# Memory keys of the sample group: from 128x128 turns on TensorE to 32x32 turns on VectorE, with scores in 32x32 tiles

## The chip, the cores and the metric

The kernel runs on one core of a Trainium2 chip. The metric is the time of one execution on the device in microseconds; the kernel before is stated by the median of its runs, and one further execution was profiled.

## What is computed

One layer of a hybrid decoder, for a prompt of 512 rows and a sample group of 8 sequences with 4 rows each, with the same weights: a mixer (mLSTM and differential attention), a cross-attention into 256 memory tokens, and a gated feed-forward part with a short convolution. The change lies in the cross-attention of the sample group. Its keys and values come from caches, 256 tokens by 4 heads by 256 features for each sequence:

```python
def mem_attend(h, mk, mv, w_mq, w_mo):
    B, T, _ = h.shape
    q = (h @ w_mq).reshape(B, T, MEM_HEADS, MEM_HEAD_DIM)
    s = jnp.einsum('bqhd,bkhd->bhqk', q.astype(jnp.float32), mk.astype(jnp.float32)) * (MEM_HEAD_DIM ** -0.5)
    p = jax.nn.softmax(s, axis=-1)
    o = jnp.einsum('bhqk,bkhd->bqhd', p, mv.astype(jnp.float32)).reshape(B, T, D_MODEL)
    return o.astype(h.dtype) @ w_mo
```

## The kernel before

Rows are worked in blocks of 128 partitions: four blocks of the prompt, and one block of 32 rows (`NS`) for the sample group. Large matrix products take the prompt's weights and activations as two parts each (a rounded part and a rest), three products for each; the sample group is computed in plain f32, which TensorE works off as two records for each product.

The instructions of each engine are in one order, made ahead of time: a scheduler goes through the program as written, and takes an instruction that stands later when an earlier one has to wait for its operands or for a free buffer. Buffers come from pools. The ones that matter here:

- `stg` ("st", 6 buffers of 128x1024 f32): staging for everything that is loaded, weights and cached keys alike.
- `wp` ("W", 4 buffers, each twice as large): weights after their split, the turned keys `kT`, and the cached values `vt`.
- `psm` ("mm", 5 banks) and `psa` ("at", 3 banks): the accumulators of TensorE.
- `zp` (3 buffers) and `t2p` (8 buffers): the prompt's probabilities, and what they become when turned.

The stage that the change touches runs like this. The queries of both groups are projected by `gemmB` in eight blocks of 128 features (`ev_q` takes each out of its bank; block m of the sample group lands in `qs[:, m, :]`). The first four blocks are done with all weights at hand, the last four one after the other, and behind each of these two tiles of 128 cached memory tokens are loaded (`mk_load`) and turned (`mk_turn`): eight transposes of 128x128 on TensorE against the identity (L1387), four to a bank, and each bank is copied to `kT` by ScalarE or VectorE (L1388). Each sequence has two such tiles. A loop over the eight sequences then computes scores (`mk_scores`, L1397): for each of two halves of the features and each head a product with 128 features on the rows, the 32 sample rows as weights, and 256 tokens as moving columns; the four heads stand at partitions 0, 32, 64 and 96 of one bank. `sample_exp` takes a maximum over the 256 tokens (L1014) and an exponential with its sum (L1015). All 32 rows meet all eight sequences; the pairs that don't belong together are masked out later, in `sample_softmax`, which joins the eight results into `az`. The weighted sums (`mv_out`, L1407) go through the cached values, loaded by `mv_load` as one 1 MB transfer a sequence.

The prompt's own cross-attention is a pipeline of eight steps, `prompt`, from which the loop takes a step here and there by `next(prompt)`: `ch_soft` (scores L1338 and their softmax), two steps later `ch_turn` (transposes L1356), one later `ch_out` (L1368, on every second step). It gives TensorE work while the sample group's softmax is under way. `NMID` steps follow the softmax of the sample group and the rest stand between the weighted sums, behind the sequences named in `VSTEPS`. The output weights `w_mo` are loaded through staging buffers into W buffers (`slotsA`), at most four ahead. After them comes the output projection.

Loads go out on SyncE's queue (SP), in the order of its instructions: a load that waits for a free buffer holds up those behind it.

Of the kernel before, what the change touches and what calls it, by code (L numbers as in the profile page):

```python
# [7 lines left out]
F32 = mybir.dt.float32  # L8
# [65 lines left out]
def kernel(ctx: ExitStack, tc: tile.TileContext, I, O):  # L74
    nc = tc.nc
# [25 lines left out]
    def N(name, w=1024):  # L101
        return npool.tile([P, 1032], F32, name=name, tag="N")[:, :w]
# [20 lines left out]
    def v2(t, b):  # L123
        return t.rearrange("p (a b) -> p a b", b=b)

    mm = nc.tensor.matmul
# [28 lines left out]
    ident = con("ident")  # L155
# [49 lines left out]
    def stage():  # L205
        return stg.tile([P, 1024], F32, name="wst", tag="st")
# [806 lines left out]
    def sample_exp(sall, b, ps, nm, su):  # L1013
        VRED(out=nm[:, b:b + 1], in_=ps, axis=AX.X, op=MAX, negate=True)  # L1014
        ACT(out=sall[:, b, :], in_=ps, func=AF.Exp, bias=nm[:, b:b + 1], accum_out=su[:, b:b + 1])  # L1015
# [289 lines left out]
        split(mvN[0][:, c], mvN[1][:, c], st)  # L1305

    qs = sm.tile([P, 8, NS], F32, name="qs", tag="qz", bufs=1)
    qh, ql = [], []

    def ev_q(m):  # L1310
        if m % 2 == 0:
            qh.append(npool.tile([P, 2, 516], F32R, name="qh", tag="N"))
        if m % 4 == 0:
            ql.append(S([P, 4, SEQ], F32R, "ql"))

        def ev(i, c0, c1, ps):
# [3 lines left out]
            STT(out=ql[m // 4][:, m % 4, c0:c0 + n], in0=ps[:, :n], scalar=1.0 / 16.0, in1=f32(q), op0=MUL, op1=SUB)  # L1320
            if i == 1:
                nc.scalar.mul(out=qs[:, m, :], in_=ps[:, n:n + NS], mul=1.0 / 16.0)
        return ev

    run(gemmB(hqT, [ev_q(m) for m in range(4)], half_first=True))
# [3 lines left out]

    def ch_soft(i):  # L1330
        h, bp = i // 2, i % 2
        sv = v2(mmp("sca"), 256)
        for j in range(2):
            t0 = (2 * bp + j) * P
            for c in range(2):
                q, l = qh[h][:, c, t0:t0 + P], ql[h // 2][:, 2 * (h % 2) + c, t0:t0 + P]
                for m, (x, k) in enumerate(((q, 0), (q, 1), (l, 0))):
                    mm(sv[:, j, :], lhsT=x, rhs=mkT[k][:, 2 * h + c, :], start=(c + m == 0), stop=(c == 1 and m == 2))  # L1338
        nm = small(2, "cnm")
        su = small(2, "csu")  # L1340
        VRED(out=nm, in_=sv, axis=AX.X, op=MAX, negate=True)
        p = cps[i] = v2(Z("cp"), 256)
        for j in range(2):
            ACT(out=p[:, j, :], in_=sv[:, j, :], func=AF.Exp, bias=nm[:, j:j + 1], accum_out=su[:, j:j + 1])
        nc.vector.reciprocal(out=su, in_=su)
        for j in range(2):
            VTS(out=p[:, j, :], in0=p[:, j, :], scalar1=su[:, j:j + 1], scalar2=None, op0=MUL)

    def ch_turn(i):
        h, bp = i // 2, i % 2  # L1350
        if bp == 0:
            pTs[h] = [[T2([P, SEQ], "pT", F32R) for _ in range(2)] for _ in range(2)]
        tp = mmp("cpt")
        for c in range(2):
            for j in range(2):
                tr(tp[:, (2 * c + j) * P:(2 * c + j + 1) * P], cps[i][:, j, c * P:(c + 1) * P], ident)  # L1356
        for c in range(2):
            split(*[p[:, 256 * bp:256 * bp + 256] for p in pTs[h][c]], tp[:, 256 * c:256 * c + 256])
# [16 lines left out]
    def mk_load(i):  # L1375
        b, c = i // 2, i % 2
        kst[i] = stage()
        dma(out=kst[i], in_=I["cache_mem_k"][0, b, c * P:(c + 1) * P].rearrange("t h d -> t (h d)"))

    def mk_turn(i):  # L1380
        b, c = i // 2, i % 2
        if c == 0:
            kts[b] = wp.tile([P, 8, 256], F32, name="kT", tag="W")
        for q in range(2):
            ps = at("tpk")
            for j in range(4):
                tr(ps[:, j * P:(j + 1) * P], kst[i][:, (4 * q + j) * P:(4 * q + j + 1) * P], ident)  # L1387
            (VCP if q else nc.scalar.copy)(out=kts[b][:, 4 * q:4 * q + 4, c * P:(c + 1) * P], in_=v2(ps, P))  # L1388

    def mk_scores(i):  # L1390
        b, c = i // 2, i % 2
        if c == 0:
            return
        ps = mmp("ssc")[:, :256]
        for c in range(2):
            for h in range(H):
                mm(ps[NS * h:NS * h + NS], lhsT=qs[:, 2 * h + c], rhs=kts[b][:, 2 * h + c, :], start=(c == 0), stop=(c == 1))  # L1397
        sample_exp(sall, b, ps, nm, su)

    def mv_load(b):  # L1400
        vts[b] = wp.tile([P, 2, DM], F32, name="vt", tag="W")
        dma(out=vts[b], in_=I["cache_mem_v"][0, b].rearrange("(c p) h d -> p c (h d)", p=P))

    def mv_out(b):
        for c in range(2):
            for h in range(H):
                mm(pso[NS * h:NS * h + NS], lhsT=az[c][:, h, b * NS:(b + 1) * NS], rhs=vts[b][:, c, 256 * h:256 * h + 256],  # L1407
                   start=(b == 0 and c == 0), stop=(b == NB - 1 and c == 1))

    sall = S([P, NB, 256], F32, "cas")  # L1410
    nm, su = small(NB, "snm"), small(NB, "ssu")
    prompt = pipe(8, ch_soft, lambda i: None, ch_turn, ch_out)

    for i in range(6):
        mk_load(i)
    for i, _ in enumerate(gemmB(hqT, [ev_q(m) for m in range(4, 8)])):
        if i % 4 == 3:
            for j in (i // 2 - 1, i // 2):
                mk_turn(j)
                mk_load(j + 6)  # L1420
    for b in range(NB):
        mk_scores(2 * b + 1)
        if b < 4:
            for j in (2 * b + 8, 2 * b + 9):
# [380 lines left out]
```

## Time and profile before

| | |
|---|---|
| median of 3 runs | 997.69 us (997.62 to 998.53) |
| profiled execution, its own time | 996.59 us |
| its span, first to last instruction | 994.8 us |
| TensorE busy | 967.3 us |
| VectorE busy | 600.0 us |
| ScalarE busy | 389.0 us |
| GpSimd busy | 194.1 us |
| moved by DMA | 130.26 MB, mean 131 GB/s |
| granted TensorE clock, mean | 0.989 |

Engines are named PE (TensorE's matmuls), PEld (its weight loads, which overlap them), DVE (VectorE), ACT (ScalarE), POOL (GpSimd) and SP (SyncE). A row of a group gives the line, the engine, the operation, the tiles written and read, the shape as partitions by elements, the count, then busy time in us and the mean duration of one in ns, and behind the second bar the idle time of the engine ahead of it with what ended it. For a matmul the shape begins with rows*columns of the array. A matmul's duration counts from its start to a modelled end, and several overlap; what one costs is seen from the length of a run of them. A row of a timeline gives the start, the length, and what ran, with the count. The queue q8 is that of TensorE's instructions.

### The profile page before, as it was taken

The page shows a single profiled execution, that of the slowest core. Times are in us where ns is not written, and L with a number is a line of the kernel's source. Part 1 is how long each engine was busy: PE and PEld are TensorE (multiplying, and loading weights), DVE is VectorE, ACT ScalarE, POOL GpSimd, SP SyncE. Part 2 cuts the span into 40 slices and gives each one's busy share as a digit, 9 for nine tenths or more (in the row PEclk, how much of TensorE's full clock was granted, in tenths as well). Part 3 has the DMA queues.
Part 4 walks back from the last instruction along what each step waited for, and adds up shares of the span by engine and source line. Part 5 has one row for each costly group of instructions (what it writes and reads, how often), then busy time and mean ns, then how long its engine had stood idle before and what let it go on. Part 6 is the DMA issues. An engine that isn't in the chain of part 4 may idle for free.

```text
span 994.8 us, 17056 instructions
## 1 busy us (share of the span) xinstructions
PE 967.3 (97%) x6615; PEld 812.5 (82%) x6615; DVE 600.0 (60%) x1129; ACT 389.0 (39%) x746; POOL 194.1 (20%) x389
## 2 busy tenths in 40 slices
PE   8999999999899999999999999999999999999994
PEld 5899777789555778898767789979987997997983
DVE  5734325643686356743653678827848685675677
ACT  5754323234376447633552444242212222222232
POOL 6610000102332124500000264301101110010115
PEclk9999999999799999999999999999999999999998
DMA  8940222352634167775851673153053213314113
GB/s 289 296 155 1 85 85 88 80 188 60 178 114 145 42 212 237 262 247 165 282 213 43 196 238 107 25 150 94 15 138 88 84 46 102 117 40 132 39 46 111
DMA packets 120401, 130.26 MB, mean 131 GB/s; under 512 B 8423, under 2 KB 85832, under 8 KB 120320
## 3 DMA queue, kind: packets, MB, share of 16 engines
q1 hardware_dynamic: 114136, 125.69, 40.6%
q10 hardware_dynamic: 6184, 3.48, 1.2%
q8 instruction: 52, 0.85, 0.4%
q14 instruction: 29, 0.24, 0.1%
HBM read 112.22 MB, written 16.93 MB: 130 GB/s over the span
## 4 chain that ended last, share of the span: by engine, by line
PE 85%; DVE 6%; DMA 5%; issue 2%; ACT 1%; POOL 1%; SPq 0%; DVEq 0%; POOLq 0%; ACTq 0%
PE mm L455 31%; PE mm L386 6%; PE mm L387 6%; PE mm L388 6%; PE mm L443 5%; PE mm L1647 4%; PE mm L1649 4%; PE mm L1648 4%; PE mm L366 3%; PE sda L1182 2%; DMA xb<-x_d 2%; PE tpk L1387 2%; PE cpo L1368 1%; PE sca L1338 1%; PE ssc L1397 1%
## 5 line engine op out<-in xcount | busy, mean ns | idle before, releaser
L142 ACT CAST wslot<-wst 128x1024 fp32r<-128x1024 f32 (+1 forms) x127 | 131.1, 1036 | 274.5 <-issue 74.4
L455 PE MATMUL mm<-fT,wslot 128*128 128x256 f32 (+1 forms) x1872 | 235.7, 288 | 0.0
L455 PEld LDWEIGHTS mm<-fT,wslot 128*128 128x128 f32 x1872 | 234.7, 188 | 0.7 <-issue 0.4
L143 DVE TENSOR_TENSOR wslot<-wst,wslot 128x1024 fp32r<-128x1024 f32 (+1 forms) x127 | 155.1, 1223 | 92.3 <-ACT wslot L142 91.7
L1647 PE MATMUL mm<-wslot,act 128*128 128x512 f32 (+1 forms) x176 | 71.0, 405 | 0.0
L1648 PE MATMUL mm<-wslot,act 128*128 128x512 f32 (+1 forms) x176 | 69.6, 395 | 0.0
L1649 PE MATMUL mm<-wslot,act 128*128 128x512 f32 (+1 forms) x176 | 69.1, 397 | 0.0
L1548 POOL COPY cvo<-u 128x2 f32<-128x2 f32 x43 | 16.1, 375 | 221.4 <-DVE u L1546 221.4
L386 PE MATMUL mm<-wslot,hT 128*128 128x512 f32 x128 | 51.8, 408 | 0.0
L455 PE MATMUL mm<-hT,wslot 128*128 128x256 f32 (+1 forms) x384 | 51.4, 290 | 0.0
L387 PE MATMUL mm<-wslot,hT 128*128 128x512 f32 x128 | 50.8, 397 | 0.0
L388 PE MATMUL mm<-wslot,hT 128*128 128x512 f32 x128 | 50.6, 398 | 0.0
L455 PEld LDWEIGHTS mm<-hT,wslot 128*128 128x128 f32 x384 | 48.9, 188 | 0.9 <-issue 0.8
L1647 PEld LDWEIGHTS mm<-wslot,act 128*128 128x128 f32 (+1 forms) x176 | 33.4, 190 | 15.8 <-issue 7.8
L1543 DVE TENSOR_TENSOR u<-mm,rsb 128x256 f32<-128x256 f32 x43 | 18.1, 423 | 43.4 <-PE mm L455 43.3
L1649 PEld LDWEIGHTS mm<-wslot,act 128*128 128x128 f32 (+1 forms) x176 | 33.0, 188 | 7.7 <-issue 0.4
L1648 PEld LDWEIGHTS mm<-wslot,act 128*128 128x128 f32 (+1 forms) x176 | 33.1, 188 | 6.4
L1560 ACT ACTIVATE c<-c 128x560 f32<-128x560 f32 x21 | 14.1, 672 | 60.2 <-DVE c L1554 60.2
L1660 DVE TENSOR_TENSOR yp<-mm,yp 128x512 f32<-128x512 f32 x40 | 27.3, 689 | 13.7 <-PE mm L1649 13.6
L1554 DVE SCALAR_TENSOR_TENSOR c<-u,cvT,c 128x560 f32<-128x560 f32 x43 | 34.3, 798 | 0.8
L1553 DVE SCALAR_TENSOR_TENSOR c<-u,cvT,c 128x560 f32<-128x560 f32 x43 | 34.1, 793 | 0.1
L386 PEld LDWEIGHTS mm<-wslot,hT 128*128 128x128 f32 x128 | 24.1, 188 | 6.6 <-issue 2.1
(458 smaller groups left out, 1876.6 us busy)
## 6 DMA issues: line engine op xcount, KB each, us to landing
wst<-in_w_up_dram SPq DMA_DIRECT2D x42, 512.0 KB
wst<-in_w_in_dram SPq DMA_DIRECT2D x28, 512.0 KB
wst<-in_w_down_dram SPq DMA_DIRECT2D x20, 512.0 KB
wst<-in_cache_mem_k_dram SPq DMA_DIRECT2D x16, 512.0 KB
vt<-in_cache_mem_v_dram SPq DMA_DIRECT2D x8, 1024.0 KB
wst<-in_w_mk_dram SPq DMA_DIRECT2D x8, 512.0 KB
xb<-in_x_prompt_dram SPq DMA_DIRECT2D x8, 512.0 KB
wst<-in_cache_dk_dram SPq DMA_DIRECT2D x16, 256.0 KB
```

Source lines behind the costliest of these rows:

```text
L142: nc.scalar.copy(out=hi, in_=src)
L143: (eng or nc.vector).tensor_tensor(out=lo, in0=src, in1=f32(hi), op=SUB)
L386: mm(ps[b], lhsT=xt.hi(k, c0, c0 + n), rhs=s[:, 0, kk, :], start=(k == 0), stop=False)
L387: mm(ps[b], lhsT=xt.hi(k, c0, c0 + n), rhs=s[:, 1, kk, :], start=False, stop=False)
L388: mm(ps[b], lhsT=xt.lo(k, c0, c0 + n), rhs=s[:, 0, kk, :], start=False, stop=(k == nk - 1))
L443: mm(ps, lhsT=s[:, l, k, :], rhs=x(k, c0, c1), start=(k == 0 and j == 0), stop=(k == 7 and j == 2))
L455: mm(ps[i], lhsT=s[:, l, k, :], rhs=x(k, c0, c1), start=(k == 0 and j == 0), stop=(k == 7 and j == 2))
L1553: STT(out=c, in0=u[:, 1:EXT - 1], scalar=w[1], in1=c, op0=MUL, op1=ADD)
L1554: STT(out=c, in0=u[:, 0:EXT - 2], scalar=w[0], in1=c, op0=MUL, op1=ADD)
L1647: mm(ps, lhsT=t[:, 0, c0:c0 + P], rhs=s[:n, 0, i % 2, :], start=st, stop=False)
L1648: mm(ps, lhsT=t[:, 0, c0:c0 + P], rhs=s[:n, 1, i % 2, :], start=False, stop=False)
L1649: mm(ps, lhsT=t[:, 1, c0:c0 + P], rhs=s[:n, 0, i % 2, :], start=False, stop=en)
```

## The change

The tile of 128 tokens by 1024 features is turned by one VectorE instruction, which turns each block of 32x32 in its place. The partitions then hold, in four groups of 32, the features of a block; the columns hold 32 blocks of features, with 32 tokens of the group in each. A product can therefore take 32 features at a time, for 32 tokens of each of two tiles (64 columns). The eight blocks of a head are summed in the bank, and each group of partitions (32 tokens of a tile) has a bank of its own: `sc[g]`, 64 columns for each sequence, held over all eight sequences. The queries must stand on every group of partitions, so `q4` gets 32 small copies from `qs`. The softmax is taken for four sequences at once (`mk_soft`): behind sequence 3, and behind sequence 7. Since four of the five `psm` banks are held, the prompt's scores and transposes move to the `psa` pool. The values of sequences 0, 1, 2 and 7 go into two staging buffers each instead of a W buffer, those of 0 to 6 are loaded inside the loop, and the prompt's steps are taken at other places.

```diff
+    q4 = N("q4").rearrange("p (r m n) -> p r m n", r=4, m=8)
...
                 nc.scalar.mul(out=qs[:, m, :], in_=ps[:, n:n + NS], mul=1.0 / 16.0)
+                if m % 4 == 3:
+                    for r in range(4):
+                        for g in range(4):
+                            cp = (nc.gpsimd.tensor_copy, VCP, nc.gpsimd.tensor_copy, nc.scalar.copy)[g]
+                            cp(out=q4[32 * g:32 * g + 32, r, m - 3:m + 1], in_=qs[32 * r:32 * r + 32, m - 3:m + 1])
...
-        sv = v2(mmp("sca"), 256)
+        sv = v2(at("sca"), 256)
...
-        tp = mmp("cpt")
+        tp = at("cpt")
...
-            kts[b] = wp.tile([P, 8, 256], F32, name="kT", tag="W")
-        for q in range(2):
-            ps = at("tpk")
-            for j in range(4):
-                tr(ps[:, j * P:(j + 1) * P], kst[i][:, (4 * q + j) * P:(4 * q + j + 1) * P], ident)
-            (VCP if q else nc.scalar.copy)(out=kts[b][:, 4 * q:4 * q + 4, c * P:(c + 1) * P], in_=v2(ps, P))
...
+            kts[b] = wp.tile([P, 2, 32, 32], F32, name="kT", tag="W")
+        nc.vector.transpose(out=kts[b][:, c].rearrange("p a b -> p (a b)"), in_=kst[i])
+
+    def mk_scores(b):
+        for j in range(8):
+            for h in range(H):
+                for g in range(4):
+                    gr = slice(32 * g, 32 * g + 32)
+                    mm(sc[g][NS * h:NS * h + NS, 64 * b:64 * b + 64], lhsT=q4[gr, j % 4, 2 * h + j // 4, :],
+                       rhs=kts[b][gr, :, 8 * h + j, :], start=(j == 0), stop=(j == 7))
+
+    def mk_soft(b0):
+        for g in range(4):
+            VRED(out=nm4[:, b0:b0 + 4, g], in_=v2(sc[g][:, 64 * b0:64 * b0 + 256], 64), axis=AX.X, op=MAX, negate=True)
+        VRED(out=nm[:, b0:b0 + 4], in_=nm4[:, b0:b0 + 4, :], axis=AX.X, op=MIN)
+        for b in range(b0, b0 + 4):
+            for g in range(4):
+                ACT(out=v2(sall[:, b, :], P)[:, :, 32 * g:32 * g + 32], in_=v2(sc[g][:, 64 * b:64 * b + 64], 32), func=AF.Exp,
+                    bias=nm[:, b:b + 1], accum_out=su4[:, b, g:g + 1])
+        VRED(out=su[:, b0:b0 + 4], in_=su4[:, b0:b0 + 4, :], axis=AX.X, op=ADD)
+
+    def mv_load(b):
+        src = I["cache_mem_v"][0, b].rearrange("(c p) h d -> c p (h d)", p=P)
+        if 2 < b < 7:
+            t = wp.tile([P, 2, DM], F32, name="vt", tag="W")
+            vts[b] = [t[:, 0], t[:, 1]]
+        else:
+            vts[b] = [stage(), stage()]
         for c in range(2):
...
+            dma(out=vts[b][c], in_=src[c])
...
+    sc = [mmp("ssc") for _ in range(4)]
+    next(prompt)
     for b in range(NB):
-        mk_scores(2 * b + 1)
+        mk_scores(b)
         if b < 4:
             for j in (2 * b + 8, 2 * b + 9):
                 mk_turn(j)
...
         else:
-            mv_load(b - 4)
-        if b % 2 == 1:
-            next(prompt, None)
+            mv_load(b - 1)
+        if b == 3:
+            for j in range(3):
+                mv_load(j)
+            next(prompt)
+            mk_soft(0)
+            next(prompt)
+    mk_soft(4)
+    next(prompt)
     _, az = sample_softmax(sall, su, None, con("selX"), "ca")
...
-    for b in range(NB):
-        if b >= 4:
-            mv_load(b)
     W.pump()
     for b in range(NB):
         mv_out(b)
+        if b == 0:
+            mv_load(7)
+        if b == 3:
+            next(prompt, None)
+            next(prompt, None)
         if b in VSTEPS:
             next(prompt, None)
```

More of the change, by code (lines that the diff above doesn't have):

```diff
@@ L1382, in mk_turn @@
         if c == 0:
-            kts[b] = wp.tile([P, 8, 256], F32, name="kT", tag="W")
-        for q in range(2):
-            ps = at("tpk")
-            for j in range(4):
[L1387 to L1394, printed above, removed]
-        for c in range(2):
-            for h in range(H):
-                mm(ps[NS * h:NS * h + NS], lhsT=qs[:, 2 * h + c], rhs=kts[b][:, 2 * h + c, :], start=(c == 0), stop=(c == 1))
-        sample_exp(sall, b, ps, nm, su)
@@ L1400, in mv_load @@
-    def mv_load(b):
-        vts[b] = wp.tile([P, 2, DM], F32, name="vt", tag="W")
-        dma(out=vts[b], in_=I["cache_mem_v"][0, b].rearrange("(c p) h d -> p c (h d)", p=P))
+            kts[b] = wp.tile([P, 2, 32, 32], F32, name="kT", tag="W")
[7 more added lines that the diff above has]
+                       rhs=kts[b][gr, :, 8 * h + j, :], start=(j == 0), stop=(j == 7))
@@ L1406, in mv_out @@
             for h in range(H):
-                mm(pso[NS * h:NS * h + NS], lhsT=az[c][:, h, b * NS:(b + 1) * NS], rhs=vts[b][:, c, 256 * h:256 * h + 256],
+                mm(pso[NS * h:NS * h + NS], lhsT=az[c][:, h, b * NS:(b + 1) * NS], rhs=vts[b][c][:, 256 * h:256 * h + 256],
                    start=(b == 0 and c == 0), stop=(b == NB - 1 and c == 1))
@@ L1411 @@
     nm, su = small(NB, "snm"), small(NB, "ssu")
+    nm4, su4 = (v2(sm.tile([P, 4 * NB], F32, name=n, tag=n, bufs=1), 4) for n in ("snm4", "ssu4"))
     prompt = pipe(8, ch_soft, lambda i: None, ch_turn, ch_out)
```

## The prediction

> **What bounds the kernel now.** I read the totals first, then the chain that ended last, then sums by stretch around the cross-attention, then single groups.
>
> ```profile
> span 994.8 us, 17056 instructions
> ...
> PE 967.3 (97%) x6615; PEld 812.5 (82%) x6615; DVE 600.0 (60%) x1129; ACT 389.0 (39%) x746; POOL 194.1 (20%) x389
> ...
> PE 85%; DVE 6%; DMA 5%; issue 2%; ACT 1%; POOL 1%; SPq 0%; DVEq 0%; POOLq 0%; ACTq 0%
> ```
>
> TensorE is busy 97% of the span and holds 85% of the chain. Time taken off it comes back as time, unless something else ends later in the stage concerned. That stage is between 434 us (second half of the query projection) and 526 us (end of the cross-attention):
>
> ```profile
> 434.00:464.50 30.50, 30.50 (x253) 30.34 (x251) 8.61 (x17) 8.67 (x22) 1.81 (x1) 1.00 0.51 157
> 464.50:491.00 26.50, 26.50 (x253) 18.26 (x252) 15.19 (x34) 12.98 (x40) 0.00 (x0) 1.00 0.71 230
> 491.00:526.00 35.00, 35.00 (x284) 23.93 (x281) 20.80 (x48) 17.80 (x55) 0.00 (x0) 1.00 0.60 223
> ```
>
> The columns are the stretch, then busy time of TensorE, weight loads, VectorE, ScalarE, GpSimd, the granted clock and the DMA share. TensorE has no gap in any of the three; VectorE has 22 us free in the first and 11 in the second. So work moved from TensorE to VectorE finds room. What the pieces cost TensorE stands in the chain, where a row is a run of one kind:
>
> ```profile
> 463.27 1.31 PE tpk L1387 x12
> ...
> 469.03 1.43 PE sca L1338 x12
> ...
> 473.61 1.00 PE ssc L1397 x16
> ...
> 491.30 2.99 PE cpo L1368 x12
> ```
>
> A key transpose costs 1.31/12 = 0.109 us, the scores of one sequence (16 records, two for each product) 1.00 us, the scores of one prompt step 1.43 us, one output pair of the prompt 2.99 us.
>
> **The change part by part.**
>
> *Transposes of the keys.*
>
> ```profile
> L1387 PE MATMUL tpk<-cpk,wst x128: 270/273/329, 439.8 to 487.5; 128*128 128x128 f32 x128
> ```
> ```profile
> L143 DVE TENSOR_TENSOR wslot<-wst,wslot 128x1024 fp32r<-128x1024 f32 x29 | 36.7, 1267 | 23.0 <-ACT wslot L142 22.9
> ...
> L1388 DVE COPY kT<-tpk 128x512 f32<-128x512 f32 x16 | 11.0, 690 | 12.8 <-PE tpk L1387 12.8
> ```
>
> 128 transposes leave TensorE: 128 x 0.109 = **14.0 us off the path**, half of it in the projection, half in the loop. Sixteen copies go from VectorE (11.0 us) and sixteen from ScalarE; both were hidden. VectorE gets 16 turns of 128x1024. No row shows one. The nearest by size is the 128x1024 subtraction, 1.27 us; two copies of 512 give 1.38. I take 1.3, with 1.1 and 2.5 as ends. Eight turns in the projection (10.4 us against 5.5 before) fit in its 22 us. Eight in the loop are 10.4 us behind each other, each pair waiting for a W buffer that the scores of an earlier sequence free.
>
> *Scores.* 64 products (128 records) of 128 rows by 256 columns become 1024 products (2048 records) of 32 rows by 64 columns. Per record a quarter of the columns, and 16 tiles of the array instead of 4 side by side, with 16 times as many records: on the array alone a sequence stays at 1.00 us. What is new is how fast records are issued and fetched.
>
> ```profile
> 323.38 0.15 PEld L1258 LDWEIGHTS ops<-ta,anew 32*32 32x32 f32 x8 [0.20 <-issue]
> ```
> ```profile
> 319.29 1.08 PE L1250 MATMUL ops<-wst,daz 128*32 128x128 f32 x32
> ...
> 323.39 0.42 PE L1258 MATMUL ops<-ta,anew 32*32 32x128 f32 x8
> ```
> ```profile
> q8 instruction: 52, 0.85, 0.4%
> ```
>
> The only 32x32 products with real columns (L1258) put 8 weight loads of some 0.10 us each within 0.15 us: starts about 7 ns apart. At 7 ns for a record, 256 records are 1.8 us. The slow end is the longest fast run, L1250: 32 records in 1.08 us, the last one 0.27, so 26 ns apart; it is held by the array, so it bounds the issue from above: 256 x 26 ns = 6.7 us for a sequence.
>
> The instruction queue moved 0.85 MB in 52 packets: 16 KB each, and TensorE's 6615 matmuls and 6615 loads are 52 times 254 instructions. So a packet is a block of some 256 instructions. Its time is 0.4% x 16 x 994.8 / 52 = 1.22 us. The new scores are 4096 instructions, 16 blocks, two for each sequence: 2.4 us, if one block comes after the other. Nothing in this trace uses blocks that fast: 52 in 995 us. [...]
>
> I take 12 of the 16 blocks at 1.22 us, four having come during the two waits ahead of the groups of four sequences (an assumption): 14.6 against 8.0 us, **+6.6**. Ends: 0 (array alone) and 8 x 5.7 = +46 (26 ns).
>
> *Query copies (q4).* 32 copies of 32 partitions, 16 of them on GpSimd, eight behind each other after the last query block. No score can start before them.
>
> ```profile
> L566 POOL CAST cb<-cpk 128x128 bf16<-128x128 f32 x1 | 0.3, 289 | 3.3 <-DMA cpk<-in_consts_dram 3.3
> ```
>
> 8 x 0.29 = 2.3 us and an evacuation of 0.6 ahead; the prompt step now placed there covers 1.43: **+1.5**, ends 0 and 3.
>
> *Softmax of four sequences at once.* It was eight times one maximum and one exponential, each hidden behind other sequences. Now each of two groups has 4 maxima, a small one, and 16 exponentials of 64 columns with their sums.
>
> ```profile
> L1014 DVE TENSOR_REDUCE snm<-ssc 128x1 f32<-128x256 f32 x8 | 3.3, 423 | 2.7 <-PE ssc L1397 2.7
> ```
> ```profile
> L1015 ACT ACTIVATE cas<-ssc,snm 128x256 f32<-128x256 f32 x8 | 3.8, 478 | 0.4 <-DVE snm L1014 0.4
> L1322 ACT ACTIVATE qs<-mm 128x32 f32<-128x32 f32 x8 | 1.6, 198 | 5.4 <-DVE ql L1320 5.4
> L1015 ACT ACTIVATION_READ_ACCUMULATOR cas<-ssc,snm 128x1 f32 x8 | 1.6, 203 | 0.0
> ```
>
> Between 198 ns for 32 columns and 478 for 256, 64 columns give 0.24 us; with the sum's read 0.44. A group is 4 x 0.42 + 0.2 + 16 x 0.44 = 8.9 us. All eight sequences write into the same four banks, so I take the second group's scores to wait until ScalarE has read the first (if only columns were compared, this term would be 0). Ahead of the first group's maxima VectorE still has the turns: from the start of the loop they end near 1.8 + 10.4 = 12 us, and the softmax near 21. TensorE has four scores (7.3), prompt steps 1 and 2 (2 x 1.43 and four transposes, 0.44: 3.3): 10.6 us. About 10 us are open; steps 3 and 4 brought forward (2 x 1.87 + 2.99 = 6.7) leave 3.3, and with what follows I take **+4**, ends 0 and 10. Everything later on TensorE, which issues in order, is queued behind those scores, and behind it both softmax chains. An idle array also gets a lower clock:
>
> ```profile
> 258.00:262.00 4.00, 3.07 (x28) 1.85 (x28) 1.13 (x5) 0.00 (x0) 3.00 (x3) 0.50 0.28 80
> ```
>
> The granted clock was 0.50 after the wait there. The second softmax stands before the weighted sums, over prompt steps that are partly used up and whose exponentials queue behind 16 others on ScalarE: **+2**, ends 0 and 6. ScalarE has 9 us more exponentials than before in this stage and 9 us fewer copies.
>
> *What the old loop lost.* From 464.5 to 491 the prices above give scores 8.0, 64 transposes 7.0, four prompt steps 5.7, eight prompt transposes 0.9: 21.6 of 26.5 us. The other 4.9 us lie between shapes and behind evacuations. The new loop has its own waits, counted above: **-4.9**.
>
> *Loads.*
>
> ```profile
> 476.36 1.58 SPq L227 DMA_DIRECT2D wst<-in_w_mo_dram  x2
> ...
> 491.45 24.14 SPq L1402 DMA_DIRECT2D vt<-in_cache_mem_v_dram  x5
> ...
> 541.62 2.36 SPq L227 DMA_DIRECT2D wst<-in_w_mo_dram  x2
> ```
>
> The values of sequences 0 to 2 and 7 now use the staging buffers, so the output weights, of which six blocks were in by 488 us, come only when the first weighted sums free them, on SP behind the values. Those are in earlier (five had trickled in until 515.6). The output projection, begun at 520 inside the attention, loses its head start: **+2**, ends -2 and 6. Sixteen issues in place of eight cost SP a few us that it has. The changed pools of the prompt's banks (three buffers instead of five) have their cost in the two waits above.
>
> **Sum.** -14.0 + 6.6 + 1.5 + 4 + 2 - 4.9 + 2 = -2.8 us, against the profiled execution's 996.59 us (1.8 outside its span): 993.8. The median of the runs, 997.69, is 1.1 above it: 994.9, so **995**.
>
> **The rivals.**
>
> *Scores as cheap as before.* If blocks are fetched well ahead, the 6.6 us vanish: 988. For it: 7 ns between starts, and 52 packets that delayed nothing. Against it: two blocks a microsecond, some forty times the mean rate. 0.22. [...]
>
> *Instruction supply at full price* (the other side). Every block waits for its fetch, p us each: 16p - 8.0 in place of 6.6, the rest of the sum being -9.4. Slower than before by 2 us from p = 1.21 on; 1.22 gives 1000, 1.5 (with a delay from request to start that no row shows) gives 1004, 1.8 gives 1009. Its place is the eight runs of scores; TensorE would stand still inside a run with nothing to wait for. For it: no row with blocks that close. Against it: blocks at hand and pauses. 0.28, at 1004.
>
> *Issue at 26 ns a record.* +46 - 9.4: 1034. The row is held by the array, L1258 speaks against it. [...] 0.08.
>
> **Chances.** The forecast has 0.38 (own range 990 to 1000); 0.04 are for more idle time than any of these. 2 us, 0.2%, are about what a measurement can tell from no change. Faster: 0.23 of the forecast, 0.21 of the cheap scores, 0.03 of the third: 0.47. Slower: 0.06, 0.18, 0.08 and 0.04: 0.36. The rest, 0.17, is no change. From 986 to 1008 the range leaves out the 26 ns, the dearest blocks and a little below.
>
> **What would show it.** Right: no tpk rows; 16 turns near 1.3 us; ssc runs of 256 records in about 1.8 us; 16 more q8 packets, less the two blocks of what is removed; a gap of TensorE ahead of the fifth sequence near 4 us, ended by ScalarE's exponentials. Wrong: runs at 1.0 us or above 2.4 us, a turn near 2.5 us, no wait at the fifth sequence, or TensorE waiting for output weights after 500 us.

## The result and the profile after

The changed kernel takes 1045.86 us (median of 4 runs, 1043.83 to 1048.32) against 997.65 for the kernel before, run beside it: a ratio of 1.0481, 95% interval 1.0459 to 1.0504. It is 48 us slower; the forecast was 995, and the range up to 1008 does not hold it. The profiled execution has a span of 1042.9 us, 48.1 more than before.

From the page of the changed kernel: totals, the queue of TensorE's instructions, the chain that ended last, and the group of the new score products.

```profile
PE 978.3 (94%) x8407; PEld 825.5 (79%) x8407; DVE 611.7 (59%) x1141; ACT 387.2 (37%) x786; POOL 198.2 (19%) x405
...
q8 instruction: 66, 1.08, 0.5%
...
PE 83%; DVE 5%; issue 4%; DMA 4%; ACT 2%; POOL 1%; SPq 0%; DVEq 0%; POOLq 0%; ACTq 0%
...
L1399 PE MATMUL ssc<-kT,q 32*32 32x64 f32 x2048 | 31.1, 282 | 31.0 <-issue 29.0
```

TensorE has more busy time than before (978.3 against 967.3 us) and 37 us more idle time. The last row holds most of both: the score products are busy for 31.1 us where eight runs of 1.00 us stood, and TensorE stood idle 31.0 us just before them, 29.0 of it ended by "issue", so that no semaphore of another engine ended it. Where that lies is seen by stretch (columns as in the prediction; before, TensorE was full at a granted clock of 1.00 in this whole time):

```profile
458.00:492.00 34.00, 18.49 (x1043) 15.68 (x1042) 14.79 (x23) 3.31 (x13) 4.13 (x9) 0.62 0.45 140
492.00:501.00 9.00, 5.82 (x35) 4.94 (x35) 5.99 (x12) 5.37 (x32) 0.00 (x0) 0.90 0.43 133
501.00:530.00 29.00, 15.29 (x1025) 13.33 (x1026) 3.59 (x13) 2.54 (x14) 0.00 (x0) 0.61 0.31 112
530.00:546.00 16.00, 11.21 (x61) 7.55 (x59) 4.24 (x13) 8.91 (x50) 0.00 (x0) 0.64 0.19 68
```

The first and third stretch are the scores of four sequences each; TensorE works half of the time, at 0.6 of its clock. The second and fourth are the two waits for the softmax. TensorE's timeline inside the first stretch shows the pattern of the loss:

```profile
469.37 1.96 PE L1399 MATMUL ssc<-kT,q 32*32 32x64 f32 x128 [1.96 <-issue]
473.37 1.98 PE L1399 MATMUL ssc<-kT,q 32*32 32x64 f32 x128 [2.05 <-issue]
477.92 1.96 PE L1399 MATMUL ssc<-kT,q 32*32 32x64 f32 x128 [2.57 <-issue]
482.47 1.99 PE L1399 MATMUL ssc<-kT,q 32*32 32x64 f32 x128 [2.60 <-issue]
```

Each of these runs is 128 records, with their 128 weight loads 256 instructions: one block of the instruction queue, by 14 packets of 16 KB more (66 against 52) for 8407 - 6615 = 1792 more matmuls and as many weight loads. (The first run of either half is longer, 150 and 254 records.) Ahead of each of the four TensorE stands still for 2.0 to 2.6 us. From start to start it is (482.47 - 469.37)/3 = 4.4 us here; the twelve full periods of both halves lie between 3.5 and 4.6 us. From 460.9, where the first run of scores starts in the chain, to 492.0, and from 501.1 to 529.5, makes 59.5 us for 16 blocks, 3.7 us a block on average with the blocks that were at hand, where 8.0 us stood: 51.5 us more. All the rest of the change is worth 48.1 - 51.5 = -3.4 us.

The first row of the output projection's matmuls, before and after, says that nothing of the difference arises later:

```profile
520.15 0.50 PE L386 MATMUL mm<-wslot,oT 128*128 128x512 f32 x1
```
```profile
568.09 0.40 PE L386 MATMUL mm<-wslot,oT 128*128 128x512 f32 x1
```

568.09 - 520.15 = 47.9 of the 48.1 us.

### The profile page after: what moved, and what is told of

It reads as the page before. It is cut to its first block, busy times and chain, and to the rows that moved or that the text cites. A ratio compares the mean times of both kernels' runs of the same rounds, so it can differ in the third digit from the quotient of the medians.

```text
span 1042.9 us, 20700 instructions
## 1 busy us (share of the span) xinstructions
PE 978.3 (94%) x8407; PEld 825.5 (79%) x8407; DVE 611.7 (59%) x1141; ACT 387.2 (37%) x786; POOL 198.2 (19%) x405
## 4 chain that ended last, share of the span: by engine, by line
PE 83%; DVE 5%; issue 4%; DMA 4%; ACT 2%; POOL 1%; SPq 0%; DVEq 0%; POOLq 0%; ACTq 0%
PE mm L455 29%; PE mm L443 6%; PE mm L386 6%; PE mm L388 6%; PE mm L387 6%; PE mm L1677 4%; PE mm L1679 3%; PE mm L1678 3%; PE ssc L1399 3%; PE mm L366 3%; PE sda L1182 2%; PE cpo L1375 1%; PE pso L1426 1%; PE oda L1208 1%; DMA xb<-x_d 1%
## 5 line engine op out<-in xcount | busy, mean ns | idle before, releaser
L142 ACT CAST wslot<-wst 128x1024 fp32r<-128x1024 f32 (+1 forms) x127 | 131.0, 1036 | 273.2 <-issue 80.1
L1399 PE MATMUL ssc<-kT,q 32*32 32x64 f32 x2048 | 31.1, 282 | 31.0 <-issue 29.0
L1399 PEld LDWEIGHTS ssc<-kT,q 32*32 32x32 f32 x2048 | 26.4, 125 | 35.7 <-issue 32.3
L1584 DVE SCALAR_TENSOR_TENSOR c<-u,cvT,c 128x560 f32<-128x560 f32 x43 | 34.3, 797 | 0.8
```

The lines of the kernel that those rows point to most:

```text
L142: nc.scalar.copy(out=hi, in_=src)
L1399: mm(sc[g][NS * h:NS * h + NS, 64 * b:64 * b + 64], lhsT=q4[gr, j % 4, 2 * h + j // 4, :], rhs=kts[b][gr, :, 8 * h + j, :], start=(j == 0) ...
L1584: STT(out=c, in0=u[:, 0:EXT - 2], scalar=w[0], in1=c, op0=MUL, op1=ADD)
```

## The experiments

The theory: score products use up their instructions faster than blocks of 256 come. A block is taken to come some 4 us after the one before it (4.4 us in the four runs above), also while TensorE works, so the cost goes with the number of instructions (a float32 product is four of them in the trace, two weight loads and two matmuls) and vanishes where a block holds 4 us of work. The rivals: each record has a price of its own; the array needs the time for its columns at a clock held down; the transfers beside the scores hold the blocks up. Each ratio compares a kernel with the kernel before on the same chip. Differences to the changed kernel's 1045.9 us go from chip to chip; the kernel before took 997.6 to 998.3 us on them.

### How many instructions, how many columns

Twice the columns for the same instructions:

```diff
-   mm(sc[g][..., 64 * b:64 * b + 64], ..., rhs=kts[b][gr, :, 8 * h + j, :], ...)
+   mm(sc[g][..., min(64 * b, 384):min(64 * b, 384) + 128], ..., rhs=kts[b][gr, :, 8 * h + (j & 6):8 * h + (j & 6) + 2, :], ...)
```

> The 1024 score products all kept, each with 128 columns in place of 64 (the second 64 belong to another feature block, so the scores are other numbers). Twice the columns, the same instructions. Instruction supply: the next block is on its way while a burst runs, so a longer burst is partly covered: 1046 to 1060 us, 15 to 16 bursts of 128 records of nearly twice the length and shorter idle between them. Columns in the array: the 16 bursts of 1.7 us double and nothing covers it, 1046 + 27 = 1073. Issue price per record: no change, 1046.

1045.08 us, ratio 1.0473 (1.0455 to 1.0490): no change. The group and the wait in this kernel:

```profile
L1399 PE MATMUL ssc<-kT,q 32*32 32x128 f32 x2048 | 36.4, 313 | 25.1 <-issue 23.3
```

Busy time is 5.3 us longer and idle time 5.9 us shorter, so the sum is what it was. The array's columns do not set the time; a price for each record would leave it as it was too.

Half the products with twice the columns:

```diff
-        for j in range(8):
+        for j in range(0, 8, 2):
...
-   mm(sc[g][..., 64 * b:64 * b + 64], ..., rhs=kts[b][gr, :, 8 * h + j, :], ...)
+   mm(sc[g][..., min(64 * b, 384):min(64 * b, 384) + 128], ..., rhs=kts[b][gr, :, 8 * h + j:8 * h + j + 2, :], ...)
```

> Half as many score products, each twice as wide: 512 products of 128 columns in place of 1024 of 64. Each takes in 64 columns that belong to another feature block, so the scores are other numbers; the columns that pass the array are as many as in the changed kernel. Instruction supply (a block of 256 TensorE instructions takes about 4.1 us to come, one block at a time): 8 blocks go, 1046 - 8 x 4.1 = 1013 us, and the score records still come in bursts of 128 with 1.5 to 2.5 us of idle between them. A price of each record's issue (26 ns): 1024 records go, 1046 - 27 = 1019, without bursts. Columns in the array at a clock held down (the array's own time): 1046, no change.

1016.86 us, ratio 1.0191 (1.0174 to 1.0208). All 1024 products, read as bf16, one weight load and one matmul for each:

```diff
-    q4 = N("q4").rearrange(...)
+    q4 = N("q4").bitcast(bfloat16)[:, :1024].rearrange(...)
...
-                       rhs=kts[b][gr, :, 8 * h + j, :], ...)
+                       rhs=kts[b].bitcast(bfloat16)[gr, :, 8 * h + j, 1::2], ...)
```

> Queries and turned keys of the score products read as bf16 (the upper halves of the same words; the rounding differs, the products are the same 1024). A float32 product is two weight loads and two matmul records in the trace, a bf16 product one of each. Instruction supply: 2048 instructions, 8 blocks of 256 in place of 16: 1046 - 8 x 4.1 = 1013 us, the same as with half the products of twice the width, though here the products are all there; bursts still of 128 records. Issue price of 26 ns per record: 1046 - 27 = 1019. Array's own time: 1046 minus at most half to three quarters of 16 x 1.7, 1026 to 1032.

1015.39 us, ratio 1.0170 (1.0153 to 1.0187). Full runs of 128 records take 1.30 to 1.35 us here, 1.96 in the changed kernel: a third less; half to three quarters was taken off for the array's own time. Both have 8 blocks instead of 16, and 58 packets on the instruction queue instead of 66; one has twice the columns of the other at four-byte width, and they differ by 1.5 us. The eight blocks are worth (1045.9 - 1016.9)/8 = 3.6 and (1045.9 - 1015.4)/8 = 3.8 us each. But 26 ns for each of the 1024 records less gives 1019, which is as near: these times tell the array's columns off, not the price of a record.

### What else moves

The transfers of keys and values left out:

```diff
-        nc.vector.transpose(..., in_=kst[i])
+        nc.vector.transpose(..., in_=kst[i % 6])
...
-            dma(out=vts[b][c], in_=src[c])
...
-                mk_load(j + 6)
...
+        vts[b] = [kts[NB - 1][:, c].rearrange("p a b -> p (a b)") for c in range(2)]
```

> The cached keys are loaded for the first six half sequences only and turned again for the others, and the cached values aren't loaded (the turned keys stand in their place), so scores and output are other numbers; no key or value transfer runs beside the score products. Theory that a block's 4.1 us is the round trip itself: bursts and idle as before, period 3.8 to 4.1 us, 1046 less what the loads held up at the end (0 to 4 us), so 1040 to 1046. Theory that the fetches are held up by the loads on the DMA engines (0.3 to 0.4 of them busy): the period falls to 2.5 to 3 us, 1046 - 16 x 1.3 = 1025.

1044.20 us, ratio 1.0452 (1.0427 to 1.0476). TensorE's timeline from 507 us on, and the DMA totals with the moved GB/s in 40 slices of 507 to 529 us (0.55 us each):

```profile
511.13 1.96 PE L1399 MATMUL ssc<-kT,q 32*32 32x64 f32 x128 [1.50 <-issue]
514.58 1.95 PE L1399 MATMUL ssc<-kT,q 32*32 32x64 f32 x128 [1.50 <-issue]
518.31 1.96 PE L1399 MATMUL ssc<-kT,q 32*32 32x64 f32 x128 [1.77 <-issue]
```
```profile
GB/s 0 0 0 30 0 0 0 0 0 30 0 0 0 0 0 0 30 0 0 0 0 0 30 0 0 0 0 0 30 0 0 0 0 0 0 30 0 0 0 0
DMA packets 6, 0.10 MB, mean 4 GB/s; under 512 B 0, under 2 KB 0, under 8 KB 0
...
q8 instruction: 6, 0.10, 1.8%
```

These six packets of 16 KB are all that moves in 22 us, and the runs still come every (518.31 - 511.13)/2 = 3.6 us. The third packet starts at 515.9 in the trace, 1.3 us after a run's start at 514.58; it takes about 1.8% x 16 x 22 / 6 = 1.1 us, and the next run starts at 518.31, some 1.3 us after the packet's end. So a block's moving time is a third of its period; the rest stands before and behind it. The loads are not the main cause, but the period is longer beside them (below). The total shows little of it, because in the first half of this kernel loads of output weights came in their place (there two periods are 4.8 and 5.1 us). The twelve full periods of the changed kernel average 4.0 us, against 3.6 here: by that, an estimate, some 6 of the 51.5 us. A period of the changed kernel with hardly any transfer, and one of the kernel with bf16 products in the middle of the loads (a run of 1.30 us and the wait behind it):

```profile
482.47:485.93 3.46, 1.99 (x129) 1.74 (x129) 1.91 (x2) 0.00 (x0) 0.00 (x0) 0.50 0.02 5
```
```profile
472.70:478.65 5.95, 1.30 (x129) 1.14 (x129) 3.43 (x4) 0.00 (x0) 0.00 (x0) 0.50 0.89 306
```

With the DMA engines 0.89 busy a block took 5.9 us here, with 0.02 it took 3.5.

### A price for each record, or for each block

A step of the prompt behind every sequence:

```diff
     for b in range(NB):
...
         if b == 3:
...
-            next(prompt)
             mk_soft(0)
-            next(prompt)
+        next(prompt)
     mk_soft(4)
-    next(prompt)
...
-    for _ in range(NMID):
-        next(prompt, None)
```

> The same products, but a step of the prompt's attention stands behind every sequence instead of in four places, so that about 6 us of slow TensorE work lies between every two blocks of score instructions. Instruction supply: a block can come while the prompt's matmuls run, about half of the 16 round trips are covered in part, 1046 - 8 x 2 = 1030 us (1025 to 1036). Issue price per record, or the array's own time: where the products stand doesn't matter, 1046.

1036.20 us, ratio 1.0385 (1.0360 to 1.0409): 9.7 us less with every record in place, just above the upper end of what block supply gave (1025 to 1036); the wait ended by issue fell from 29.0 to 19.0 us.

```profile
PE ssc L1399 <- issue: 19.0, 9, 3.6
```

Then work was added. First a matmul behind every four products:

```diff
                     mm(sc[g][...], ...)
+                mm(dum[:, :256], lhsT=mkT[0][:, j, :P], rhs=mkT[0][:, j, :], start=True, stop=True)
```

> Work is added: behind every 4 score products stands one matmul of 128 rows by 256 columns whose result nobody reads (one pass, about 0.12 us; 32 for each sequence, 256 in all, 31 us of TensorE work and two more blocks of instructions). Instruction supply: the added work runs while the next block is on its way, so most of it is free: idle shrinks in place of the work, 18 blocks of 4.0 us in place of 16, 1046 + 8 = 1054 us at most. A price of each record's issue, or the array's own time: the added work comes on top, 1046 + 31 = 1077.

1163.63 us, ratio 1.1658 (1.1634 to 1.1683): neither theory's number. The group and the timeline:

```profile
L1400 PE MATMUL ssc<-kT,q 32*32 32x64 f32 x2048 | 89.2, 286 | 4.3 <-issue 4.3
```
```profile
475.63 0.44 PE L1400 MATMUL ssc<-kT,q 32*32 32x64 f32 x8
476.00 0.58 PE L1402 MATMUL dum<-mkT 128*128 128x256 f32 x1
476.51 0.44 PE L1400 MATMUL ssc<-kT,q 32*32 32x64 f32 x8
476.88 0.58 PE L1402 MATMUL dum<-mkT 128*128 128x256 f32 x1
```

Nearly all of the idle for instructions is gone (29.0 to 4.3 us), since a block now lasts over 10 us. But the whole-array matmul starts 0.37 us after the start of the group of eight records, and the next group 0.51 us after it: 0.88 us for nine records, at a granted clock of 0.50, where records inside a run of one shape lie 13 ns apart. So half as many of these matmuls were added, eight in a row behind every 64 products:

```diff
+            for i in range(8 if j % 4 == 3 else 0):
+                mm(dum[:, :256], lhsT=mkT[0][:, i, :P], rhs=mkT[0][:, i, :], start=True, stop=True)
```

> The added matmuls again (128 rows by 256 columns, results unread), but eight in a row behind every 64 score products, so that the shape of the array changes twice for each block and not every four products: 16 groups, by the spacing in the run before 0.2 us each at the clock of 0.5 (1.7 us a group) and about 0.4 us for the change of shape, 34 us of work in all, and one block of instructions more. Instruction supply: a block's 64 products and its eight fillers together last 3.7 us and the next block comes meanwhile, so the fillers go where the idle was: 1046 to 1056 us, idle ended by issue down from 29 to 10 us or less. Price for each record: 34 us on top, 1075 to 1080, whatever the idle.

1052.10 us, ratio 1.0544 (1.0523 to 1.0565). The groups between 455 and 540 us, and the timeline:

```profile
L1400 PE MATMUL ssc<-kT,q 32*32 32x64 f32 x2048 | 30.3, 268 | 17.6 <-issue 17.5
L1403 PE MATMUL dum<-mkT 128*128 128x256 f32 x128 | 24.6, 351 | 1.9 <-ACT cp L1351 1.6 <-issue 0.2
```
```profile
517.07 2.30 PE L1400 MATMUL ssc<-kT,q 32*32 32x64 f32 x128
519.30 2.08 PE L1403 MATMUL dum<-mkT 128*128 128x256 f32 x8
521.30 2.14 PE L1400 MATMUL ssc<-kT,q 32*32 32x64 f32 x128
```

TensorE got 24.6 us of work and the kernel became 6.2 us longer, as block supply said (1046 to 1056; a price for each record said 1075 to 1080). Where a run and its added work together lasted 4.2 us, as from 517.07 to 521.30, there is no idle time at all: here work of 4.2 us hid a block. Issue idle fell to 17.5 us, not to 10 or less, for two reasons. The scheduler did not keep all of the added work where it was written: 34 of the 128 matmuls ran in front of the first long run of scores and 16 in one go at 504.46, behind the pause, so that early runs of scores had none behind them, and three waits of 1.8 to 2.8 us stand there as before. These 50 matmuls took 6.8 us outside of the gaps, about what the kernel lost. And in some places eight matmuls took 1.2 us instead of 2.1 (from 523.37 and from 526.91), and waits of 0.7 and 0.8 us for instructions stand in the runs behind them.

### The rest of the change

One of eight feature blocks alone:

```diff
-        for j in range(8):
+        for j in range(1):
```

> Only the first of the eight feature blocks is multiplied (128 products in place of 1024, 256 records, 2 blocks of instructions); seven eighths of each score are left out, everything else of the change stays. Instruction supply: 1046 - 14 x 4.1 = 989 us, and what is left is what all the rest of the change is worth beside the kernel before (about -9 us). Issue price of 26 ns per record: 1046 - 1792 x 0.026 = 999. If the loss lay in the waits for the softmax or in the later loads, most of it stays: 1030 or more.

1000.28 us, ratio 1.0017 (1.0007 to 1.0027). 14 blocks less are worth 45.6 us, but the remainder is 2 us slower than before and not 9 faster. TensorE's waits between 455 and 505 us:

```profile
PE cpt L1363 <- DVE cp L1354: 9.1, 2, 6.5
PE cpo L1375 <- ACT cas L1408: 3.2, 1, 3.2
PE ssc L1399 <- ACT cas L1408: 1.7, 1, 1.7
```

14 us of idle time, most of which the changed kernel, with its gaps in the scores, does not have: 9.1 for VectorE's multiplication in the prompt's softmax, 4.9 for the exps. To find what holds VectorE, the turns alone, in the kernel before:

```diff
-        for q in range(2):
-            ps = at("tpk")
-            ... (transposes and copies)
+        nc.vector.transpose(out=kts[b][:, 4 * c:4 * c + 4, :].rearrange("p a b -> p (a b)"), in_=kst[i])
```

> The kernel before with one edit: VectorE's 32x32 turns in place of the 128 transposes on TensorE and their 32 evictions; the old score products read the keys in the wrong order, so scores are other numbers. What the removal alone is worth: 997.7 - 14.0 = 984 us if TensorE bounds this stage throughout (128 x 0.109 us), up to 990 if the turns of 1.22 us or the loads come to bound it in places.

990.11 us, ratio 0.9924 (0.9902 to 0.9946): 7.9 us instead of 14. TensorE's wait, and VectorE's timeline ahead of its end:

```profile
PE cpt L1356 <- DVE cp L1347: 5.8, 1, 5.8
```
```profile
469.85 0.13 DVE L1345 RECIPROCAL csu<-csu 128x2 f32<-128x2 f32 x1
469.89 0.40 DVE L1014 TENSOR_REDUCE snm<-ssc 128x1 f32<-128x256 f32 x1
470.21 1.24 DVE L1384 STREAM_TRANSPOSE kT<-wst 128x1024 f32<-128x1024 f32 x1
...
472.27 2.35 DVE L1384 STREAM_TRANSPOSE kT<-wst 128x1024 f32<-128x1024 f32 x2
474.55 0.39 DVE L1014 TENSOR_REDUCE snm<-ssc 128x1 f32<-128x256 f32 x1
474.86 0.60 DVE L1347 TENSOR_SCALAR cp<-cp,csu 128x256 f32<-128x256 f32 x2
```

The reciprocal is done at 470, the multiplication behind it starts at 474.9: three turns and four maxima (three of the sample group, one of the prompt) stand between them in VectorE's order. The test of it, eight late turns left out:

```diff
     def mk_turn(i):
+        if i >= 8:
+            return
...
-                mm(ps[...], lhsT=qs[:, 2 * h + c], rhs=kts[b][:, 2 * h + c, :], ...)
+                mm(ps[...], lhsT=qs[:, 2 * h + c], rhs=kts[b % 4][:, 2 * h + c, :], ...)
```

> The kernel before with turns on VectorE in place of the transposes, as in the run that measured the removal alone (990.1 us), but the eight turns among the score products are left out; sequences five to eight read the keys of one to four. Theory: those turns stand in VectorE's queue ahead of the prompt's softmax multiplications, which TensorE awaits for 5.8 us; without them the wait goes, 990.1 - 5.8 = 984 us, which is the whole 14 us of the transposes. Rival: the 14 us are cut short by something else (the clock held down after it, the key loads): 988 to 990, with the wait still there or another in its place.

980.58 us, ratio 0.9823 (0.9798 to 0.9848). The wait is gone, and more came back than forecast, 9.5 us. In the stretch 460 to 500 us, the turns alone and then without the late ones:

```profile
460.00:500.00 40.00, 33.80 (x301) 25.01 (x296) 30.05 (x65) 18.66 (x70) 0.00 (x0) 0.91 0.73 255
```
```profile
460.00:500.00 40.00, 40.00 (x383) 28.63 (x381) 25.41 (x66) 21.48 (x79) 0.00 (x0) 1.00 0.88 321
```

6.2 us of idle time and a granted clock of 0.91 instead of 1.00 (another 3 us, an estimate, by 33.8 x 0.09) make up nearly all of the 9.5. So the late turns kept the transposes from being worth all of their 14 us. (This run does half of the turns not at all and holds no W buffers for them, so cached values are loaded earlier too; in neither run did TensorE wait for a load here.)

The two pauses for the softmax were tried twice. Both softmaxes behind the last sequence:

```diff
             next(prompt)
-            mk_soft(0)
             next(prompt)
+    mk_soft(0)
     mk_soft(4)
```

> The softmax of the first four sequences is moved behind the last sequence's products, beside the softmax of the other four; the same numbers come out. The score products of sequences five to eight then wait for no exps. If the first pause (about 9 us before the fifth sequence, of which some 6 us are work of the prompt) is worth its idle share, the time falls by 2 to 6 us and the second pause grows by up to as much as the exps of four more sequences take (16 x 0.6 = 9 us on ScalarE): 1040 to 1050 us. If instruction supply alone carries the loss, the change is within 3 us of 1046.

1047.73 us, ratio 1.0508 (1.0478 to 1.0537): nothing, as its wait for issue is 31.0 us and the pause moved to the end. And one shift for four sequences:

```diff
-        VRED(out=nm[:, b0:b0 + 4], ..., axis=AX.X, op=MIN)
-        for b in range(b0, b0 + 4):
-            for g in range(4):
-                ACT(out=...[:, :, 32 * g:32 * g + 32], in_=v2(sc[g][:, 64 * b:64 * b + 64], 32), ..., accum_out=su4[:, b, g:g + 1])
+        VRED(out=nm[:, b0:b0 + 1], ..., axis=AX.XY, op=MIN)
+        for g in range(4):
+            ACT(out=...[:, :, 32 * g:32 * g + 32], in_=v2(sc[g][:, 64 * b0:64 * b0 + 256], 32), func=AF.Exp, bias=nm[:, b0:b0 + 1])
+        VRED(out=su[:, b0:b0 + 4], in_=sall[:, b0:b0 + 4, :], axis=AX.X, op=ADD)
```

> The changed kernel (f32, 16 blocks) with one shift for four sequences: 4 exps of 256 columns in place of 16 of 64, one VectorE sum of 1024 columns in place of 16 accumulations. It measures what the two pauses for the softmax cost in the changed kernel: the pause of 9.0 us ahead of the fifth sequence ends with its exps (3.85 us in the chain of work), the second has 4.75 us of them. If they end the pauses, 4 to 6 us go: 1040 to 1042. If the pauses are filled by the prompt's steps and the block that is fetched meanwhile, nothing: 1044 to 1048.

1038.28 us, ratio 1.0404 (1.0378 to 1.0431): 7.6 us off, beyond the 4 to 6 expected. So the exps of the pauses were on the path.

### Fewer blocks, with everything done

Two sequences' keys as bf16 beside each other in one tile, so that one product of two instructions serves two sequences (4 blocks); then with the prompt's steps behind each pair and ahead of the late turns; then with one shift as above:

```diff
+            kts[b // 2] = wp.tile([P, 2, 2, 32, 32], bfloat16, name="kT", tag="W")
+        nc.vector.transpose(out=kts[b // 2][:, b % 2, c]..., in_=kst[i].bitcast(bfloat16)[:, 1::2])
...
+                    mm(sc[g][..., 64 * b:64 * b + 128], lhsT=q4[...], rhs=kts[b // 2][gr, :, :, 8 * h + j, :], ...)
```

> Queries and turned keys as bf16 (the turn reads the upper halves of the words), two sequences side by side in one tile, so that one product of 128 columns serves two sequences: 512 products of two instructions, 4 blocks of 256 in place of 16; turns, softmax and the prompt's steps stay where they are. Instruction supply: from 1015.4 us with 8 blocks another 4 x 2.7 to 4 x 3.7 off, 1001 to 1005; below that the wait for VectorE's turns takes over (1000.3 with 2 blocks). If the price sat in the columns or in the tiles of the array: 1015, no change from 8 blocks.

> As the pairs, with a step of the prompt's attention behind every pair of sequences and ahead of the late turns in VectorE's queue. Theory: the wait of 6 us for the prompt's multiplications behind the turns goes, and about 2 us of each of three blocks are covered: 1003 - 6 - 4 = 993 us, 990 to 998. Rival: the turns then come late themselves and the score products wait for them (four turns of 1.2 us, 5 us at one place or two): 1000 or more.

> As the pairs spread out, with one shift (the least of four sequences' negated maxima) for four sequences, so that 4 exps of 256 columns stand for 16 of 64, and one VectorE sum for 16 accumulations. ScalarE's 16 x 0.6 = 9.6 us become about 4 x 0.5 = 2 us twice; the waits for exps ahead of the fifth sequence and of the sample output shrink by what of them is still uncovered: 2 to 5 us less than the pairs spread out, unless VectorE's sum of 1024 columns (about 1.1 us) takes it back.

996.74 us (0.9988, 0.9973 to 1.0004), 995.34 (0.9977, 0.9963 to 0.9990) and 991.23 (0.9934, 0.9913 to 0.9955). The pairs came below their forecast: one wait for instructions, 3.0 us, is left in that kernel, so the other blocks arrived during other work, and none of its waits is for the prompt's multiplication. The prompt ahead of the turns then had little left to give. In the last kernel, the score group:

```profile
L1402 PE MATMUL ssc<-kT,q 32*32 32x128 bf16 x512 | 8.3, 255 | 4.1 <-issue 2.2 <-DVE ql L1322 1.1 <-ACT q L1329 0.7
```

It beats both kernels, with queries and keys cut to bf16 for the scores, though by 0.7% only: the scores are busy for 8.3 us, near the 8.0 that eight runs of 1.00 took before the change, and one wait of 2.2 us for instructions is left.

## Why the prediction was wrong

**The step that failed is the price of a block.** The prediction counted 16 blocks rightly (14 more packets, 66 against 52, with the two blocks of what was removed), and took the time of a packet, 1.22 us, for the time that a block costs, for 12 of them. The packet's time was right: 1.6% x 16 x 26 / 6 = 1.1 us here, by the six packets between 465 and 491 us.

```profile
q8 instruction: 6, 0.10, 1.6%
```

But a block costs from one start to the next, about 4 us, of which the packet is a third. The row from which 1.22 came says how long the queue is busy, not how long the engine is without instructions, and in the old trace packets start at least 11.5 us apart, so none of its blocks was used up in 2 us. The term is +51.5 us instead of +6.6. The assumption that four blocks would be at hand fell too: TensorE's waits from 455 to 545 us have 14 for instructions, in 16 blocks, so two were at hand.

```profile
PE ssc L1399 <- issue: 29.0, 14, 2.6
```

**The rival that had it right in kind** was instruction supply at full price, by 16p - 8.0 - 9.4. It put p at 1.5 to 1.8 us with "a delay from request to start"; with the 3.7 us measured it gives +41.8, where the kernel lost 48. The run with work added by the block bears it out: 29.0 us of idle time in 16 blocks in the changed kernel, and none where a block and its added work lasted 4.2 us.

**26 ns for each record** gave 1034, nearest of all rivals to the time, by luck: inside a run records lie (1.96 - 0.31)/127 = 13 ns apart at half the clock, and the rest of the time is one wait behind each 128. That 13 ns was itself mis-sized at 7: runs of 128 records took 1.6 to 2.0 us, where 256 were forecast in 1.8.

**The turns.** 1.22 us each against 1.3 forecast, so the room on VectorE was judged rightly and the order was not: work on VectorE was not hidden there. In the kernel before, the eight late turns took back 9.5 of the 17.6 us that came off without them. In the changed kernel TensorE's waits show none for the multiplications behind the turns; that this price lies under the gaps of the scores is argued, from the run with one of eight blocks, and was not tested by itself.

```profile
L1391 DVE STREAM_TRANSPOSE kT<-wst x16: 1200/1218/1246, 439.3 to 494.1; 128x1024 f32<-128x1024 f32 x16
```

**Transposes and the old loop's losses**, -14.0 and -4.9, agree as a sum with the run without the late turns: 17.6 us against 18.9. Its first scores start 5.9 us earlier than before (7.0 was forecast for the projection), and the rest came in the loop, where the run does not separate the two terms.

**The softmax pauses**, +4 and +2. The places were right: TensorE stands idle 9.00 - 5.82 = 3.2 us in the first pause and 16.00 - 11.21 = 4.8 us in the second. The exps were mis-sized: 0.36 us and 0.25 for the sum instead of 0.24 and 0.20.

```profile
L1408 ACT ACTIVATE cas<-ssc,snm x32: 303/355/406, 497.1 to 536.0; 128x64 f32<-128x64 f32 x32
L1408 ACT ACTIVATION_READ_ACCUMULATOR cas<-ssc,snm x32: 198/250/301, 497.3 to 536.2; 128x1 f32 x32
```

By the run with one shift, 7.6 us of the two pauses came off the path, more than the two terms' 6 together, and a wait of 1.1 us for exps was left.

**Loads and output weights**, +2: nothing after the attention, by the two rows of the output projection above; what loads cost, they cost by a longer wait for blocks (periods of 4.0 us on average, against 3.6 without them). The query copies' +1.5 wasn't tested by itself; waits on them in the score group come to under 1 us.

All terms but the scores made -9.4 and came to -3.4 in the changed kernel. The 6 us between are pauses and turns, partly under the gaps; how they divide there was not measured.

## What to carry to other kernels

Count TensorE's instructions as the trace does (four for a float32 product, two for a bf16 one), divide by 256, and see how long each block works: here a block with less than about 4 us of work cost 3.5 to 4.6 us, with twice the columns in it 3.5 to 4.8, and up to 5.9 us beside heavy transfers. The cut into small tiles made 2048 records of 128 here, busy for 31.1 us instead of 8.0, with 29.0 us of waits for instructions. Twice the columns took from that where the products were halved (1016.9 us against 1045.9) and nothing where they were not (1045.1); bf16 products took from it (1015.4), both together, with two sequences in a product, left 3.0 us of waits for instructions (996.7 us), and where a block and its added work lasted 4.2 us no wait was left. And work moved to an engine with free time was not free where something that TensorE awaits stood behind it in that engine's order: the eight late turns took back 9.5 us of 17.6.

## What the hardware showed that was not expected

- Blocks of 256 TensorE instructions, used up in 2 us, came every 3.5 to 4.6 us, and every 3.5 to 4.0 with no other traffic (5.9 us in the kernel with bf16 products, with the DMA engines 0.89 busy); a packet was under way for about 1.1 us of that. In the changed kernel's trace no two of these packets overlap, and the closest start 3.4 us apart; what fills the other two thirds was not found.
- The granted clock was 0.6 while TensorE stood idle half of the time, and it was 0.50 with TensorE busy in 40.0 of 40 us, in the kernel with a matmul of 128 rows behind every four products:

```profile
500.00:540.00 40.00, 40.00 (x413) 22.02 (x414) 2.37 (x2) 0.00 (x0) 0.00 (x0) 0.50 0.14 44
```

- One matmul on the whole array between every four products in 32x32 tiles cost 118 us for 256 added matmuls, 0.46 us each. Eight of them in a row took 521.30 - 519.30 = 2.0 us where they were slow, 0.25 us each; with 0.1 us for the eight records, some 0.5 of the 0.88 us of a group is left, at the two changes of shape, an estimate.
- VectorE turned 128x1024 in 32x32 blocks in 1.22 us as float32, and in 1.21 us as bf16 (the row is from the kernel of pairs with the prompt's steps spread out).

```profile
L1391 DVE STREAM_TRANSPOSE kT<-wst 128x1024 bf16<-128x1024 bf16 x16 | 18.5, 1214 | 4.1 <-PE mm L455 4.1
```
